# Norms whose second four outputs take x * g, with the memory's norm among the gate products

## The chip, the core and the metric

The kernel runs on one core of one Trainium2 chip. The time is that of one execution on the device, in microseconds (us). A core has a matrix engine (PE, which loads weights beside its matmuls as PEld), a vector engine (DVE), a scalar engine (ACT), a general engine (POOL), and queues that issue transfers (SP and others). Each engine runs its own instructions in order and waits on semaphores for the others.

## The reference, cut to what matters

Two blocks run one after the other on 256 rows of width 1024. The first mixes three branches (window attention, spatial gating, pooling), then attends to a memory, then has a feed-forward layer. The second puts 16 rows in front (272 in all), and has a recurrent mixer, a gated feed-forward layer with a convolution, an attention with stick-breaking weights, and a second such feed-forward layer. What the change touches:

```python
def rmsnorm(x, g):
    y = xf * lax.rsqrt(jnp.mean(xf * xf, axis=-1, keepdims=True) + EPS)
    return (y * g.astype(jnp.float32)).astype(x.dtype)
...
        h = rmsnorm(x, g_norm[l, 0])
        q, k, v, su, sv, pc, gate = split_columns(h @ w_in[l])
        ya = window_sink_attention(q, k, v, attn_sinks[l])
        yb = spatial_gating(su, sv, g_sgu[l], w_spatial[l], b_spatial[l])
        yc = multiscale_pool(pc, w_pool[l], pool_scale[l])
        proj = jnp.einsum('bsnc,ncd->bsnd', branches, w_branch[l])
        gates = jax.nn.sigmoid(gate.reshape(B, S, N_BRANCH, D_MODEL))
        merged = jnp.sum(gates * proj, axis=2)
        x = x + rmsnorm(merged @ w_out[l], g_norm[l, 1])
        hm = rmsnorm(x, g_norm[l, 2])
        mem_n = rmsnorm(mem, g_mem[l])
...
        hf = rmsnorm(x, g_norm[l, 4])
        yf = jnp.square(jax.nn.relu(hf @ w_up[l])) @ w_down[l]
...
        h = h + conv_glu_ffn(rms_norm(h, norm_ffn_g[layer]), ffn_up[layer], ffn_conv_w[layer],
                             ffn_conv_b[layer], ffn_down[layer])
```

Since 1 / rms is one number for each row of x, (x * g * r) @ w is the same as ((x * g) @ w) * r: a product can be started before r is known and scaled as it leaves PSUM.

## The kernel before

Activations lie feature-major: 128 partitions, 8 chunks of features (kc), and 256, 258 or 272 columns, one for each row of x. One output `ft` of a product is 128 features, summed over 8 kc in a PSUM bank. Each of these blocks is three matmuls (`mm3`): x and w are both split in a high and a low part (xh and xl, whi and wlo), and hi*hi, lo*hi and hi*lo are added up (lines 388, 389, 390). Weights come in groups of 8 blocks; ACT casts a group to whi, DVE subtracts wlo. A group listed in `W.whole` is used as it arrives, as one matmul of full width (L385, which the profile shows as two records), without cast and subtraction; it lies in a buffer of whi or wlo, which is why those names stand in its rows.

`Norm` prepares a product that begins with a norm. `steps` writes x * g (`raw`; named xh and xl, or xg in whole groups) and adds up squares in `acc`. `first` then computes the first four outputs from `raw`, chunk by chunk (`outer`: for each kc all four outputs), while a matmul with ones (L436, the colsum) and ACT give r = `rstd`. The first four leave PSUM through DVE (`ev` = ps * r). For the outputs behind them `split` makes `dst`, the normed x: nt = x * g * r on DVE, its high part xh on ACT, its low part xl on DVE. The second four (`then`) take `dst`, again chunk by chunk, and the ninth output and all others take it one output after the other (`dense`). Four norms have a second four: w_in (256 columns, split weights), w_up (256, whole), f_up0 (272, whole), f_up1 (258, split). WHOLE names the first group of w_up and of f_up0, and four groups from there are whole.

After w_in come 24 gate products (w_in 18 to 41), and after each of them three steps of side work: attention (eight blocks, each a chain of scores, reduces `am`, exponentials and scaling of `p`, transposes to `pT`, a product and the split to yah and yal), gating and pooling, by turns (`together`). Then the 24 branch products run in the order of outputs of n=1 and 2 by turns, then n=0 (which takes ya); `ev_merge` multiplies each with its gate on DVE and adds them up to `merged`, which w_out takes. Beside these products norm_mem makes `memn`, the normed memory. It has its buffer from h0 (the `dst` of w_in), so it can only write once the last gate product is done.

The order of the instructions on each engine is set as the program is built, by a scheduler that follows dependences and its own estimates, so a step given at another place in the code can land at another place on each engine.

Of the kernel before, what the change touches and what calls it, by code (L numbers as in the profile page):

```python
# [18 lines left out]
P = 128  # L19
# [245 lines left out]
def interleave(jobs, side, per=1):  # L265
    for job in jobs:
        job()
        for _ in range(per):
            next(side, None)
# [7 lines left out]
def together(*gens):  # L277
    gens = list(gens)
    while gens:
        for g in list(gens):  # L280
            try:
                next(g)
                yield
            except StopIteration:
                gens.remove(g)
# [3 lines left out]
def model(ctx: ExitStack, tc: tile.TileContext, a: dict, out: bass.AP, stage=None):  # L289
# [54 lines left out]
    W = Weights(nc.nc if WRAW else nc, a["wblk"], rawp, hlp, 2, 1)  # L344
    W.after = after
    for first in WHOLE:
        W.whole.update(range(first, first + 4))

    h = const.tile([P, KC, T], F32, name="h")
    vec = const.tile([P, NVEC], F32, name="vec")  # L350
# [61 lines left out]
    def xpair(n, k=KC, tag="x", bufs=2, pool=xp):  # L412
        xh = pool.tile([P, k, n], F32R, tag=tag + "h", name=tag + "h", bufs=bufs)
        xl = pool.tile([P, k, n], F32R, tag=tag + "l", name=tag + "l", bufs=bufs)
        return xh, xl
# [40 lines left out]
    class Norm:  # L456
# [33 lines left out]
        def first(self, items, then=(), ahead=None):  # L490
            def rstd():
                self.r = rstd_of(self.sums, self.n)

            assert not self.whole or len(W.order) // BLK_G in WHOLE
            tiles = outer([x[:2] for x in items], self.raw, self.n, 2, ahead, rstd)
            W.hold = []
            nc.stop()
            dst = xpair(self.n) if then else None
            for i, ((_, ft, ev), ps) in enumerate(zip(items, tiles)):
                if then:  # L500
                    self.split(dst, range(4 * i, 4 * i + 4) if i < 2 else ())
                    if i == 0:
                        table["hold"] += casts
                t = ep[0].tile([P, T], F32, tag="ev", name="ev")[:, :self.n]
                vtt(t, ps, self.r, op=ALU.mult)
                ev(ft, t)
            if then:
                for (_, ft, ev), ps in zip(then, outer([x[:2] for x in then], dst, self.n, 1)):
                    ev(ft, ps)
            return dst  # L510

        def split(self, dst, ks):
# [2 lines left out]
    def outer(items, x, n, nd=2, ahead=None, late=None):  # L515

        tiles = [(pd.tile([P, 512], F32, tag="pd", name="pd") if i < nd else pss.tile([P, 512], F32, tag="sc", name="sc"))[:, :n] for i in range(len(items))]
        for kc in range(KC):
            if ahead is not None:
                next(ahead)  # L520
            if kc == KC - 1 and late is not None:
                late()
            for (name, ft), ps in zip(items, tiles):
                mm3(ps, W.blocks([(name, kc, ft)]), x[0][:, kc, :], x[1][:, kc, :], kc == 0, kc == KC - 1)
        return tiles
# [16 lines left out]
    with tc.tile_pool(name="b1", bufs=1) as b1, tc.tile_pool(name="b2", bufs=2) as b2:  # L542
# [61 lines left out]
        def attention():  # L604
            ps = pss.tile([P, 2, 128], F32, tag="sc", name="sc")
            for i in range(2):
                nc.tensor.transpose(ps[:, i, :], vT[:, i * 128:(i + 1) * 128], ident)
            nc.scalar.copy(vtok, ps)
            yield
            for qt in (1, 0):  # L610
                nk = 128 * (qt + 1)
                for j in range(4):
                    sc = [pss.tile([P, 256], F32, tag="sc", name="sc")[:, :nk] for _ in range(2)]
                    mk = cmask[:, 128:384] if qt else cmask[:, 384:512]
                    for hh in range(2):
                        mm(sc[hh], lhsT=cmask[:, 0:128], rhs=mk, start=True, stop=False)
                    for hh in range(2):
                        r = slice(hh * 64, hh * 64 + 64)
                        mm(sc[hh], lhsT=qT[r, j, qt * 128:qt * 128 + 128], rhs=kT[r, 0:nk], start=False, stop=True)
                    yield  # L620
                    m = wk.tile([P, 4, 2], F32, tag="am", name="am")
                    for hh in range(2):
                        nc.vector.tensor_reduce(m[:, 0, hh:hh + 1], sc[hh], axis=AX.X, op=ALU.max)
                    vtt(m[:, 0, :], m[:, 0, :], sinks[:, j, :], op=ALU.max)
                    vts(m[:, 1, :], m[:, 0, :], -1.0, None, op0=ALU.mult)
                    vtt(m[:, 2, :], sinks[:, j, :], m[:, 0, :], op=ALU.subtract)
                    act(m[:, 2, :], m[:, 2, :], AF.Exp)
                    p = b2.tile([P, 2, 256], F32, tag="p", name="p")
                    for hh in range(2):
                        act(p[:, hh, :nk], sc[hh], AF.Exp, bias=m[:, 1, hh:hh + 1], accum_out=m[:, 3, hh:hh + 1])  # L630
                    vtt(m[:, 3, :], m[:, 3, :], m[:, 2, :], op=ALU.add)
                    nc.vector.reciprocal(m[:, 3, :], m[:, 3, :])
                    for hh in range(2):
                        vts(p[:, hh, :nk], p[:, hh, :nk], m[:, 3, hh:hh + 1], None, op0=ALU.mult)
                    yield
                    tp = pss.tile([P, 2, 2, 128], F32, tag="sc", name="sc")
                    for hh in range(2):
                        for kt in range(qt + 1):
                            nc.tensor.transpose(tp[:, hh, kt, :], p[:, hh, kt * 128:kt * 128 + 128], ident)
                    pT = b2.tile([P, 2, 2, 128], F32, tag="pT", name="pT")  # L640
                    nc.scalar.copy(pT[:, :, 0:qt + 1, :], tp[:, :, 0:qt + 1, :])
                    yield
                    o = pss.tile([P, 128], F32, tag="sc", name="sc")
                    for hh in range(2):
                        for kt in range(qt + 1):
                            mm(o[hh * 64:hh * 64 + 64, :], lhsT=vtok[:, kt, hh * 64:hh * 64 + 64], rhs=pT[:, hh, kt, :],
                               start=kt == 0, stop=kt == qt)
                    yield
                    ts_ = slice(qt * 128, qt * 128 + 128)
                    split(ya[0][:, j, ts_], ya[1][:, j, ts_], o)  # L650
                    yield
# [39 lines left out]
        def pooling():  # L691
            pool = b1.tile([P, 4, S], F32, name="pool")
            for g in range(4):
                src = cpad[:, g, :]
                for i in range(g + 1):
                    d = 1 << i
                    lo = 2 * d - 1
                    dst = b2.tile([P, 16 + S], F32, tag="psum", name="psum")
                    vtt(dst[:, lo:], src[:, lo:], src[:, lo - d:16 + S - d], op=ALU.add)
                    src = dst  # L700
                vtt(src[:, 16:32], src[:, 16:32], ptab[:, g, :], op=ALU.mult)
                stt(pool[:, g, :], src[:, 16:], 0.5 ** (g + 1), cpad[:, g, 16:], op0=ALU.mult, op1=ALU.subtract)
                yield
            for g in range(4):
                ps = pss.tile([P, S], F32, tag="sc", name="sc")
                mm(ps, lhsT=wpool[:, g, :], rhs=pool[:, g, :], start=True, stop=True)
                yield
                y = ep[0].tile([P, T], F32, tag="nt", name="nt")[:, :S]
                act(y, ps, AF.Copy, scale=vcol("pool_scale", g))
                split(yc[0][:, g, :], yc[1][:, g, :], y)  # L710
                yield

        nc.sync.dma_start(mem, a["memT"])
        jobs = [dense("w_in", 18 + i, KC, h0, S, ev_in) for i in range(24)]
        side = together(attention(), gating(), pooling())
        interleave(jobs, side, 3)
        drain(side)

        merged = xpair(S)
        memn = xpair(S)  # L720

        def norm_mem():
            acc = new_acc(S)
            for kc in range(KC):
                sumsq(mem[:, kc, :], acc, kc == 0, S)
            yield
            r = rstd_of([acc], S)
            for kc in range(KC):
                norm_split(lambda kc: mem[:, kc, :], "g_mem", 0, S, r, memn, (kc,))
                yield  # L730

        mg = {}

# [10 lines left out]
                    stt(merged[1][:, ft, :], mg[ft], 0.5, merged[0][:, ft, :], op0=ALU.mult, op1=ALU.subtract)  # L744
            return ev

        side = norm_mem()
        order = [(n, ft) for fts in (range(NBR), range(NBR, 8)) for ns in ((1, 2), (0,)) for ft in fts for n in ns]
        interleave([dense(f"w_br{n}", ft, 4, (ya, yb, yc)[n], S, ev_merge(n)) for n, ft in order], side)
        drain(side)  # L750

    def add_post(post, steps, width, stop, pool=(), ready=1, fill=0):

# [1086 lines left out]
```

## Time and profile before

| | us |
|---|---|
| median of 3 runs | 1325.83 |
| lowest and highest | 1320.94, 1328.16 |
| the profiled execution | 1322.63 |
| its span | 1320.9 |
| busy PE, DVE, ACT, POOL | 1268.0, 894.8, 705.6, 178.5 |

The span is the time from the first to the last instruction in the profile; the rest of the execution's own time lies around it. [...]

### The profile page before, as it was taken

The page shows a single profiled execution, that of the slowest core. Times are in us where ns is not written, and L with a number is a line of the kernel's source. Part 1 is how long each engine was busy: PE and PEld are TensorE (multiplying, and loading weights), DVE is VectorE, ACT ScalarE, POOL GpSimd, SP SyncE. Part 2 cuts the span into 40 slices and gives each one's busy share as a digit, 9 for nine tenths or more (in the row PEclk, how much of TensorE's full clock was granted, in tenths as well). Part 3 has the DMA queues.
Part 4 walks back from the last instruction along what each step waited for, and adds up shares of the span by engine and source line. Part 5 has one row for each costly group of instructions (what it writes and reads, how often), then busy time and mean ns, then how long its engine had stood idle before and what let it go on. Part 6 is the DMA issues. An engine that isn't in the chain of part 4 may idle for free.

```text
span 1320.9 us, 25715 instructions
## 1 busy us (share of the span) xinstructions
PE 1268.0 (96%) x10188; PEld 1176.1 (89%) x10188; DVE 894.8 (68%) x1812; ACT 705.6 (53%) x1349; POOL 178.5 (14%) x237
## 2 busy tenths in 40 slices
PE   5999998999999989999999999999999999899997
PEld 5999998888999976877877679999999989899997
DVE  6576586857664457567486468786567557989954
ACT  6566555675554434433242256665457666666643
POOL 1000000000000000434211002553000000135500
PEclk9999999998999999999999989999999999999999
DMA  7554455433555653432202125555554333655663
GB/s 257 157 175 134 155 149 162 153 128 128 178 190 179 188 192 120 128 96 65 71 13 64 50 65 166 170 176 178 175 170 142 125 95 87 191 171 178 191 182 106
DMA packets 54984, 188.16 MB, mean 142 GB/s; under 512 B 7598, under 2 KB 9792, under 8 KB 54736
## 3 DMA queue, kind: packets, MB, share of 16 engines
q1 hardware_dynamic: 53856, 185.27, 44.6%
q8 instruction: 80, 1.31, 0.4%
q0 software_dynamic: 464, 0.73, 0.3%
q10 hardware_dynamic: 544, 0.52, 0.1%
q14 instruction: 40, 0.33, 0.1%
HBM read 185.56 MB, written 1.05 MB: 141 GB/s over the span
## 4 chain that ended last, share of the span: by engine, by line
PE 84%; DVE 10%; ACT 3%; DMA 1%; issue 1%; POOL 1%; SPq 0%; DVEq 0%; ACTq 0%; POOLq 0%
PE pd L388 19%; PE pd L390 19%; PE pd L389 19%; PE pd L385 9%; PE l L986 3%; PE f L986 2%; DVE wlo L214 2%; PE sc L389 1%; PE sc L390 1%; PE sc L385 1%; DVE sh L214 1%; PE sc L388 1%; PE s L986 1%; DVE nt L214 1%; PE sc L1608 1%
## 5 line engine op out<-in xcount | busy, mean ns | idle before, releaser
L214 DVE TENSOR_TENSOR wlo<-raw,whi 128x1024 fp32r<-128x1024 f32 x270 | 332.5, 1233 | 208.6 <-ACT whi L214 204.1
L214 ACT CAST whi<-raw 128x1024 fp32r<-128x1024 f32 x298 | 312.2, 1049 | 299.4 <-PE pd L389 201.4
L388 PE MATMUL pd<-xh,whi 128*128 128x256 f32 (+2 forms) x1264 | 364.0, 289 | 18.9 <-ACT xh L214 12.4
L389 PE MATMUL pd<-xl,whi 128*128 128x256 f32 (+2 forms) x1264 | 361.2, 286 | 6.3 <-DVE xl L214 6.3
L390 PE MATMUL pd<-xh,wlo 128*128 128x256 f32 (+2 forms) x1264 | 361.0, 287 | 0.7 <-DVE wlo L214 0.6
L388 PEld LDWEIGHTS pd<-xh,whi 128*128 128x128 f32 x1264 | 241.8, 192 | 22.8 <-ACT xh L214 13.8
L389 PEld LDWEIGHTS pd<-xl,whi 128*128 128x128 f32 x1264 | 242.6, 192 | 7.4 <-DVE xl L214 7.2
L390 PEld LDWEIGHTS pd<-xh,wlo 128*128 128x128 f32 x1264 | 242.2, 192 | 1.6 <-DVE wlo L214 1.2
L389 PE MATMUL pd<-gl,whi 128*128 128x272 f32 (+1 forms) x352 | 100.1, 285 | 0.0
L388 PE MATMUL pd<-gh,whi 128*128 128x272 f32 (+1 forms) x352 | 100.0, 285 | 0.0
L390 PE MATMUL pd<-gh,wlo 128*128 128x272 f32 (+1 forms) x352 | 99.9, 284 | 0.0
L214 DVE SCALAR_TENSOR_TENSOR c<-pd,vec,c 128x256 f32<-128x256 f32 (+3 forms) x148 | 72.0, 487 | 13.6 <-ACT c L214 11.9
L214 POOL TENSOR_TENSOR wlo<-raw,whi 128x1024 fp32r<-128x1024 f32 x28 | 67.2, 2401 | 77.4 <-ACT whi L214 77.4
L390 PE MATMUL pd<-uh,wlo 128*128 128x256 f32 x256 | 72.5, 283 | 0.4 <-DVE wlo L214 0.4
L388 PE MATMUL pd<-uh,whi 128*128 128x256 f32 x256 | 72.6, 284 | 0.0
L389 PE MATMUL pd<-ul,whi 128*128 128x256 f32 x256 | 72.4, 283 | 0.0
L214 POOL TENSOR_TENSOR s<-s,c 128x272 f32<-128x272 f32 (+1 forms) x44 | 41.9, 953 | 191.3 <-ACT s L214 191.3
L390 PEld LDWEIGHTS pd<-gh,wlo 128*128 128x128 f32 x352 | 66.3, 188 | 0.0
L389 PEld LDWEIGHTS pd<-gl,whi 128*128 128x128 f32 x352 | 66.3, 188 | 0.0
L388 PEld LDWEIGHTS pd<-gh,whi 128*128 128x128 f32 x352 | 66.2, 188 | 0.0
L214 POOL MEMSET hn<- 128x8 f32 x1 | 0.1, 147 | 479.5 <-PE sc L436 479.5
L214 DVE TENSOR_TENSOR gl<-c,gh 128x272 fp32r<-128x272 f32 (+1 forms) x44 | 56.4, 1284 | 1.1 <-ACT gh L214 1.1
(443 smaller groups left out, 2650.8 us busy)
## 6 DMA issues: line engine op xcount, KB each, us to landing
raw<-in_wblk SPq DMA_DIRECT2D x298, 512.0 KB, 3.6
whi<-in_wblk SPq DMA_DIRECT2D x24, 512.0 KB, 3.5
wlo<-in_wblk SPq DMA_DIRECT2D x24, 512.0 KB, 3.6
mem<-in_memT SPq DMA_DIRECT2D x1, 1024.0 KB, 6.7
h<-in_xT SPq DMA_DIRECT2D x4, 128.0 KB, 5.5
h<-in_xT POOLq DMA_DIRECT2D x4, 128.0 KB, 6.5
out<-h SPq DMA_DIRECT2D x2, 256.0 KB, 2.4
out<-h ACTq DMA_DIRECT2D x2, 256.0 KB, 2.5
```

The costliest lines, as they stand in the source:

```text
L214: ins = f(*args, **kw)
L385: first = mm(ps, lhsT=wh, rhs=xh, start=start, stop=stop)
L388: first = mm(ps, lhsT=wh, rhs=xh, start=start, stop=False)
L389: mm(ps, lhsT=wh, rhs=xl, start=False, stop=False)
L390: W.used(mm(ps, lhsT=wl, rhs=xh, start=False, stop=stop))
L986: latest[:] = [nc.tensor.matmul(*args, **kw)]
L1608: mm(z[hh][:, c0:c0 + n], lhsT=k[j][r, s0:s0 + 128], rhs=q[j][r, q0 - Q0:], start=False, stop=True, skip_group_check=True)
```

## The change

Eight groups instead of four are whole at w_up and f_up0. In all four norms the second four outputs are computed one after the other from x * g, and leave PSUM through an `ev` on DVE as the first four do; only the ninth output and those behind it take `dst`. norm_mem follows gating in the side work of the gate products, and the branch products have no side work. `memn` is taken before `merged`, so it lies where x * g of w_in was.

```diff
     for first in WHOLE:
-        W.whole.update(range(first, first + 4))
+        W.whole.update(range(first, first + 8))
...
             dst = xpair(self.n) if then else None
+
+            def scaled(ft, ev, ps):
+                t = ep[0].tile([P, T], F32, tag="ev", name="ev")[:, :self.n]
+                vtt(t, ps, self.r, op=ALU.mult)
+                ev(ft, t)
+
             for i, ((_, ft, ev), ps) in enumerate(zip(items, tiles)):
...
-                t = ep[0].tile([P, T], F32, tag="ev", name="ev")[:, :self.n]
-                vtt(t, ps, self.r, op=ALU.mult)
-                ev(ft, t)
-            if then:
-                for (_, ft, ev), ps in zip(then, outer([x[:2] for x in then], dst, self.n, 1)):
-                    ev(ft, ps)
+                scaled(ft, ev, ps)
+            old = bank["dense"]
+            for i, (name, ft, ev) in enumerate(then):
+                if i in (1, 2):
+                    bank["dense"] = lambda: pss.tile([P, 512], F32, tag="sc", name="sc")
+                dense(name, ft, KC, self.raw, self.n, lambda ft, ps: scaled(ft, ev, ps))()
+                bank["dense"] = old
             return dst
...
         jobs = [dense("w_in", 18 + i, KC, h0, S, ev_in) for i in range(24)]
-        side = together(attention(), gating(), pooling())
-        interleave(jobs, side, 3)
-        drain(side)
-
-        merged = xpair(S)
         memn = xpair(S)
...
+        side = together(attention(), both(gating(), norm_mem()), pooling())
+        interleave(jobs, side, 3)
+        drain(side)
+
+        merged = xpair(S)
...
-        side = norm_mem()
         order = [(n, ft) for fts in (range(NBR), range(NBR, 8)) for ns in ((1, 2), (0,)) for ft in fts for n in ns]
-        interleave([dense(f"w_br{n}", ft, 4, (ya, yb, yc)[n], S, ev_merge(n)) for n, ft in order], side)
-        drain(side)
+        for n, ft in order:
+            dense(f"w_br{n}", ft, 4, (ya, yb, yc)[n], S, ev_merge(n))()
```

How instructions move, first on DVE at the norm of w_in. Before, from the eviction of the first four (`ev`) on, DVE has the rest of the split in one piece, with the subtractions of the next weights behind it (`acc` is the memory's sum of squares):

```order
L214 TENSOR_TENSOR wlo<-raw,whi 128x1024
L214 TENSOR_TENSOR xl<-nt,xh 128x256 x4
L214 TENSOR_TENSOR acc<-acc,sq 128x256
L214 SCALAR_TENSOR_TENSOR nt<-h,vec,rstd 128x256 x4
L214 TENSOR_TENSOR xl<-nt,xh 128x256 x4
L214 TENSOR_TENSOR wlo<-raw,whi 128x1024 x6
```

In the change the same place, from that `acc` on, reads:

```order
L214 TENSOR_TENSOR acc<-acc,sq 128x256
L214 TENSOR_TENSOR ev<-pd,rstd 128x256
L214 TENSOR_TENSOR ev<-sc,rstd 128x256
L214 SCALAR_TENSOR_TENSOR nt<-h,vec,rstd 128x256
L214 TENSOR_TENSOR wlo<-raw,whi 128x1024
L214 SCALAR_TENSOR_TENSOR nt<-h,vec,rstd 128x256 x3
L214 TENSOR_TENSOR ev<-sc,rstd 128x256
L214 TENSOR_TENSOR wlo<-raw,whi 128x1024
L214 TENSOR_TENSOR xl<-nt,xh 128x256
L214 TENSOR_TENSOR ev<-pd,rstd 128x256
L214 TENSOR_TENSOR wlo<-raw,whi 128x1024
L214 TENSOR_TENSOR xl<-nt,xh 128x256
```

Behind it come two reduces of the first attention block and the last two xl. So the second half of the split stands among evictions and subtractions. Next PE at w_up, from the colsum (`acc,ones` of 256 columns) on. Before, the second four take the normed x, chunk by chunk:

```order
L436 MATMUL sc<-acc,ones 128x256
L388 MATMUL pd<-xh,whi 128x256
L388 MATMUL sc<-xh,whi 128x256 x3
L436 MATMUL sc<-acc,ones 128x16
L389 MATMUL pd<-xl,whi 128x256
L390 MATMUL pd<-xh,wlo 128x256
```

In the change:

```order
L436 MATMUL sc<-acc,ones 128x256
L385 MATMUL pd<-xg,wlo 128x256 x2
L385 MATMUL sc<-xg,wlo 128x256 x2
L385 MATMUL pd<-xg,whi 128x256 x5
L385 MATMUL sc<-xg,wlo 128x256 x8
L385 MATMUL sc<-xg,whi 128x256 x8
L385 MATMUL pd<-xg,wlo 128x256 x8
L388 MATMUL pd<-xh,whi 128x256
```

The last row is the ninth output's first; the second four now stand ahead of every product of the split x. Last DVE at the end of the n=1 and 2 branch products. Before, the last attention block's scaling of p and its yal lie between merges (`gates`), and the first nt of the memory follows:

```order
L214 TENSOR_SCALAR p<-p,am 128x128 x2
L214 SCALAR_TENSOR_TENSOR gates<-gates,pd 128x256
L214 TENSOR_TENSOR wlo<-raw,whi 128x1024
L214 SCALAR_TENSOR_TENSOR gates<-gates,pd 128x256
L214 TENSOR_TENSOR gates<-gates 128x256
L214 TENSOR_TENSOR wlo<-raw,whi 128x1024
L214 TENSOR_TENSOR yal<-sc,yah 128x128
L214 SCALAR_TENSOR_TENSOR gates<-gates,pd 128x256 x2
L214 SCALAR_TENSOR_TENSOR nt<-mem,vec,rstd 128x256 x4
```

In the change the merges of n=1 and 2 end with the first two rows here, and the whole last block follows, from its reduces to its yal, ahead of the first merge of n=0:

```order
L214 TENSOR_TENSOR gates<-gates 128x256
L214 TENSOR_TENSOR wlo<-raw,whi 128x1024
L214 TENSOR_TENSOR yal<-sc,yah 128x128
L214 TENSOR_REDUCE am<-sc 128x1 x2
L214 TENSOR_TENSOR am<-am,sinks 128x2
L214 TENSOR_SCALAR am<-am 128x2
L214 TENSOR_TENSOR am<-sinks,am 128x2
L214 TENSOR_TENSOR am<-am 128x2
L214 RECIPROCAL am<-am 128x2
L214 TENSOR_SCALAR p<-p,am 128x128 x2
L214 TENSOR_TENSOR yal<-sc,yah 128x128
L214 SCALAR_TENSOR_TENSOR gates<-gates,pd 128x256 x2
```

On PE, 21 matmuls of n=0 products stand between this block's scores and its transposes, and nothing but its own product between these and the next n=0 rows. Over the whole program DVE has 8 subtractions of wlo fewer and 16 ev more, ACT 8 casts of whi fewer and two table loads more (15 instead of 13).

## Rows read from the trace of the kernel before

**Rows 1.** The page, its first part: busy time, share of the span, instructions.

```profile
PE 1268.0 (96%) x10188; PEld 1176.1 (89%) x10188; DVE 894.8 (68%) x1812; ACT 705.6 (53%) x1349; POOL 178.5 (14%) x237
```

**Rows 2.** Timeline of PE, first norm: start, length, instruction, count, idle time before and releaser.

```profile
25.30 0.28 PE L390 MATMUL sc<-xh,wlo 128*128 128x256 f32 x1
27.88 0.38 PE L388 MATMUL pd<-xh,whi 128*128 128x256 f32 x1 [2.31 <-ACT xh L214]
...
31.69 0.58 PE L389 MATMUL pd<-xl,whi 128*128 128x256 f32 x1 [3.07 <-DVE xl L214]
...
45.20 0.28 PE L388 MATMUL pd<-xh,whi 128*128 128x256 f32 x1
```

**Rows 3.** Windows: busy PE, PEld, DVE, ACT, POOL (instructions), clock, DMA share, GB/s.

```profile
32.00:37.00 5.00, 5.00 (x25) 5.00 (x25) 3.90 (x11) 2.45 (x5) 0.00 (x0) 0.50 0.31 105
60.00:80.00 20.00, 20.00 (x168) 19.92 (x167) 16.20 (x25) 11.22 (x17) 0.00 (x0) 1.00 0.60 184
100.00:140.00 40.00, 40.00 (x331) 38.02 (x331) 24.31 (x46) 26.83 (x57) 0.00 (x0) 1.00 0.46 137
194.00:212.00 18.00, 13.36 (x102) 12.17 (x100) 14.81 (x35) 7.82 (x16) 0.00 (x0) 1.00 0.36 117
307.00:313.00 6.00, 5.70 (x26) 5.59 (x27) 6.00 (x18) 3.72 (x9) 0.00 (x0) 0.50 0.04 17
786.00:790.00 4.00, 4.00 (x19) 4.00 (x20) 4.00 (x12) 1.96 (x5) 0.00 (x0) 0.50 0.38 131
1130.00:1149.00 19.00, 18.97 (x159) 18.76 (x157) 19.00 (x34) 14.33 (x25) 3.13 (x4) 1.00 0.56 168
```

**Rows 4.** Timeline of DVE, first norm.

```profile
25.69 1.23 DVE L214 TENSOR_TENSOR wlo<-raw,whi 128x1024 fp32r<-128x1024 f32 x1 [0.33 <-ACT whi L214]
26.84 1.67 DVE L214 SCALAR_TENSOR_TENSOR nt<-h,vec,rstd 128x256 f32<-128x256 f32 x4
28.42 0.75 DVE L214 TENSOR_TENSOR ev<-pd,rstd 128x256 f32<-128x256 f32 x2
...
34.48 1.43 DVE L214 TENSOR_TENSOR xl<-nt,xh 128x256 fp32r<-128x256 f32 x4
```

**Rows 5.** Timeline of PE, w_up.

```profile
289.02 1.13 PE L385 MATMUL pd<-xg,whi 128*128 128x256 f32 x4 [0.24 <-ACT xg L214]
...
302.93 0.59 PE L436 MATMUL sc<-acc,ones 128*128 128x256 f32 x2
305.50 0.39 PE L388 MATMUL pd<-xh,whi 128*128 128x256 f32 x1 [1.97 <-ACT xh L214]
...
321.54 0.28 PE L388 MATMUL pd<-xh,whi 128*128 128x256 f32 x1
```

**Rows 6.** Timeline of PE, f_up0.

```profile
780.75 1.08 PE L385 MATMUL sc<-xg,wlo 128*128 128x272 f32 x4
...
785.75 0.60 PE L389 MATMUL pd<-xl,whi 128*128 128x272 f32 x1 [2.90 <-DVE xl L214]
...
799.95 0.29 PE L388 MATMUL pd<-xh,whi 128*128 128x272 f32 x1
```

**Rows 7.** Timeline of PE, f_up1.

```profile
1152.53 0.36 PE L388 MATMUL pd<-xh,whi 128*128 128x258 f32 x1 [3.56 <-DVE c L214]
```

**Rows 8.** Waits of PE in 184 to 216: us in total, times, longest.

```profile
PE pd L388 <- DVE gates L214: 2.8, 4, 1.4
PE pd L388 <- ACT y L214: 1.2, 1, 1.2
```

**Rows 9.** Timeline of ACT, first norm.

```profile
28.96 1.28 ACT L214 ACT_TABLE_LOAD   x1
```

**Rows 10.** Timeline of DVE, the last attention block.

```profile
177.12 0.48 DVE L214 TENSOR_REDUCE am<-sc 128x1 f32<-128x128 f32 x2
...
182.41 0.48 DVE L214 TENSOR_SCALAR p<-p,am 128x128 f32<-128x128 f32 x2
...
188.49 0.29 DVE L214 TENSOR_TENSOR yal<-sc,yah 128x128 fp32r<-128x128 f32 x1 [1.84 <-ACT yah L214]
```

## The prediction

> **What bounds the kernel now.** I read the page first: the matrix engine (PE) is busy 96% of the span [rows 1], so only three things can move the time: work on PE, gaps on PE, and stretches in which PE runs at half its clock. The timeline of PE at the places where the change works, and the windows around them, then show where gaps and half clock are.
>
> At the first norm (w_in) the first four outputs end at 25.58 us (25.30 + 0.28). PE then waits 2.31 us for ACT's xh and, after four products, 3.07 us for DVE's xl, and the ninth output starts only at 45.20 [rows 2]. That is 19.6 us for 32 blocks. At full clock a split block is three matmuls at 20.00 / 168 = 0.119 us [rows 3], so 32 blocks need 11.4 us. [...] What PE waits for is the chain on DVE: nt from 26.84, the evictions, then xl until 35.9 [rows 4].
>
> The same happens at w_up: the colsum ends at 303.53 (302.93 + 0.59, two records), the second four start at 305.50, and the ninth output at 321.54 [rows 5]; the clock is 0.50 in 307 to 313 [rows 3]. And at f_up0: end at 781.83, a wait of 2.90 at 785.75, ninth output at 799.95 [rows 6], with 0.50 in 786 to 790 [rows 3]. At f_up1 there is no such wait: DVE is busy 19.00 of 19 us behind it, and PE loses 3.56 us later, at 1152.53, to a PSUM bank that DVE's c rows free [rows 3, 7].
>
> The branch products are the fifth place. In 194 to 212 PE is busy 13.36 of 18.00 us [rows 3]; of the 4.6 us lost, 2.8 go to DVE's merging of gates in four waits of at most 1.4, and 1.2 to ACT's y [rows 8]. There norm_mem's nt and xl stand in DVE's queue among the merges.
>
> **The change part by part.**
>
> *First norm.* The second four no longer need xh and xl of the normed x, so PE goes on at 25.58 without a wait: 32 blocks x 0.357 = 11.4 us, to 37.0. The weights are there in time: two of the four lo halves are subtracted by 26.9 [rows 4], and by DVE's order after the other two come near 30.1 and 31.8, for outputs that PE reaches at 31.3 and 34.2. Then come the transposes of v and the first attention scores (about 1.5 us of PE work, moved here from later), so the ninth output starts near 38.5. DVE does, from 26.84 on and by the order after: nt x4 (1.67), ev x4 (1.43), a sum (0.33), wlo (1.14), xl x4 with a wlo between (1.43 + 1.14), a sum, three ev, four nt, two wlo, and so on, at 0.33 per ev, sum and xl, 0.40 per nt and 1.14 per wlo. That puts the sixth xl at 41.4 and the last two at 43.0, behind two reduces of the attention. The ninth output wants them at 40.4 and 41.1: a new wait of some 1.9 us. It ends at 43.4, where before it ended at 45.20 + 2.86 = 48.1 without the 1.5 us of attention. Gain 48.1 + 1.5 - 43.4 = **6.2 us**. Bounds: no new wait gives 8.1; a wait with a spell of half clock like that of [rows 3] (5 us lose 2.5) gives 3.7.
>
> *w_up.* These groups are now raw too. A whole block takes (302.93 - 289.02) / 32 = 0.435 us [rows 5] against 0.357 for a split one, so 32 of them cost 2.5 us more PE, and run from 303.53 to 317.4. The ninth output starts there, not at 321.54: gain **4.1 us**. The last xl stands behind the eviction of the seventh output (PE done at 313.9) and its relu, so it lands near 315.2, ahead of need; four wlo and four whi go away, four ev come. Bounds: 3 (an xl or wlo late by a us) to 4.2.
>
> *f_up0.* At 272 columns a whole block is 0.435 x 272 / 256 = 0.462 us, an estimate from [rows 5]; 32 of them are 14.8 us, and the ninth output starts at 781.83 + 14.8 = 796.6 instead of 799.95 [rows 6]: gain **3.4 us** (2.5 to 3.6).
>
> *f_up1.* No gap to remove. DVE gets four ev, 4 x 0.33 = 1.3 us, in the stretch in which it is always busy, so the wait at 1152.53 can grow by that; against it, the four outputs free their banks after one DVE instruction instead of ACT's and two of DVE's. Ends -1.5 and +1; I take **-0.9**, nearer to the full row since DVE has no slack there [rows 3]. An ev from PSUM costs what the row shows: two in 0.75 us, one every 0.33 [rows 4]. [...]
>
> *norm_mem among the gates.* It leaves the branch stage and lands, by the order after, near 100 to 140 us. DVE gets 8 nt and 8 xl, 8 x (0.40 + 0.33) = 5.9 us; it has 40 - 24.3 = 15.7 us free there. ACT gets two table loads of 1.28 [rows 9] and 8 casts of about 0.4, 5.8 us, and has 13.2 free. PE is busy all 40 us [rows 3], with three banks for its outputs to lean on. Cost 0; were the cover gone, the two table loads would show, 2.6 us.
>
> *Branch stage.* DVE is busy 14.8 us in 194 to 212, PE 13.4 [rows 3]. Of the 5.9 us of norm_mem some 4 fall there, and without them DVE has less to do than PE. That gives back the 4.6 - 1.2 = 3.4 us of waits on DVE; the wait on y stays. But the side steps are now shared with norm_mem's, and the last attention block slips: its reduces stand behind all sixteen evictions of n=1,2, and its ya is wanted by every output of n=0. Its chain, added up from [rows 10] and the rows of the same block on ACT and PE between them (reduces 0.5, small steps 0.8, exps 0.9, scaling 0.5, transposes 0.5, copies and products 1.6), is 4.7 us; 21 matmuls (2.5 us) stand beside it. New wait 2.2 us, between 0 and 9.2 (the 11.7 us that the last block took before, from 177.12 to 188.78, less the 2.5). I take 2.2, since the rows of this block now stand one behind the other on DVE. Net **+1.2** (-6 to +3.4).
>
> **Sum.** 6.2 + 4.1 + 3.4 + 1.2 - 0.9 = 14.0 us. The profiled execution took 1322.63, so 1308.6; it lies 3.2 us under the median of the runs shown (1325.83), from which the same sum gives 1311.8. I say **1310**, which is a base of 1324 less 14; the times below are from that base.
>
> **Rivals.**
> (a) *The clock falls at the new waits.* The ninth output of w_in waits 1.9 us and the last attention block 2.2; in the rows, waits of 2.31 and of 1.97 were the start of a spell at 0.50, while the waits of up to 1.4 in the branch stage left the clock at 1.00 [rows 2, 3, 5, 8]. Each spell costs about 3 us: gain 8, time 1316. [...]
> (b) *The last attention block keeps its old pace*, 11.7 us: 9.2 us of idle PE instead of 2.2, gain 7, time 1317; with a spell at half clock 1320. For it: in the trace each block takes that long. Against it: there it shares its queues with weights and gates, here not.
> (c) *The wait only moves.* If DVE, with ev, nt, xl and wlo in one queue, delivers the last xl no earlier than the ninth output started before (45.2 in w_in, 321.5 at w_up, 800.0 at f_up0), nothing is gained, and every us beyond that is lost. With the four ev more at each of the four norms (1.3 us each, 5.3 in all), less 1.2 in the branch stage, that is 1328, slower than before. For it: DVE is solid in 26.84 to 35.9 already [rows 4]. Against it: by my reckoning the last xl comes at 43.0 and 315.2, near that point at w_in but far from it at w_up.
> (d) *All goes well*: no wait at the ninth output, none at the last block, 8.1 + 4.2 + 3.6 + 3.4 = 19 us, time 1305, and 1303 with a better f_up1 and the lower base.
>
> **Chances.** Forecast 0.55 (1305 to 1315), (a) 0.20, (b) 0.10, (c) 0.07, (d) 0.08. A difference of 0.5%, 6.6 us, is about what a measurement of this kernel tells from none; the bound of faster is 1319.2. All of the forecast and of (d), most of (a) and half of (b) lie under it: 0.85. Slower, above 1332.5, takes (c) with the last block at its old pace: 0.04. Same 0.11. The range 1303 to 1320 holds all but (c) and the tails of (b) and (d).
>
> **What would show it.** In the profile after, PE goes from the first four of w_in into the second four with no idle row, at clock 1.00, and the ninth output ends near 43.4 after a wait on xl of about 2 us; at w_up the L385 rows go on for 32 blocks at 0.435 us right behind the colsum, at f_up0 likewise; no window there shows 0.50. In the branch stage one wait of PE on yal or on a transpose of p takes the place of four waits on gates. The wait on c at f_up1 is 4 to 5 us. The number of table loads is 15. The prediction is wrong if windows at 0.50 remain behind these places, if the gate products show idle PE, or if PE waits over 5 us at the last attention block.

## The result, and the profile after

The changed kernel takes 1303.11 us (median of 4 runs, 1301.97 to 1304.20) against 1323.38 us (4 runs, 1317.15 to 1328.16). The ratio is 0.9848, 95% interval 0.9818 to 0.9877: 1.5% faster, 20.3 us. Forecast were 1310 us (1303 to 1320) and a gain of 14 us. Run again later beside other kernels, the same change took 1308.71 us (1302.90 to 1313.53) against 1323.86, a gain of 15.2 us; why the same program differs by 10 us is taken up below.

The profiled execution of the change took 1302.94 us, and its span is 1301.2. Its granted clock, which the profile gives as a share of PE's full speed, is 0.995 on the mean, against 0.988 before; in the clock records of both profiles it is 1.00 or 0.50, and a window that reads otherwise holds some of each. From the page, busy time of the engines, to be set beside [rows 1]:

```profile
PE 1264.0 (97%) x10124; PEld 1169.7 (90%) x10124; DVE 889.0 (68%) x1820; ACT 700.4 (54%) x1343; POOL 181.0 (14%) x237
```

The span is 19.7 us shorter, busy PE only 4.0. To see what PE's time consists of I took two things off each span: idle PE (the span less busy PE), and busy PE times (1 less the granted clock), added up over windows of 1 us, as an estimate of what half clock costs. The rest stands for work at full clock. The estimate counts a matmul at 0.50 as twice as long as one at 1.00. At w_up before, matmuls of 256 columns start every 0.213 us at 0.50 (21 of them from 308.50 to 312.98) and every 0.119 at 1.00, 1.8 times as far apart, so there it is about an eighth too high:

```profile
312.77 0.41 PE L390 MATMUL pd<-xh,wlo 128*128 128x256 f32 x1
312.98 0.41 PE L388 MATMUL sc<-xh,whi 128*128 128x256 f32 x1
...
313.62 0.28 PE L388 MATMUL sc<-xh,whi 128*128 128x256 f32 x1
313.74 0.28 PE L389 MATMUL sc<-xl,whi 128*128 128x256 f32 x1
```

| | span | idle PE | cost of half clock | work at full clock |
|---|---|---|---|---|
| before | 1320.9 | 52.9 | 12.1 | 1255.9 |
| the change | 1301.2 | 37.2 | 3.3 | 1260.7 |
| difference | -19.7 | -15.7 | -8.8 | +4.8 |

The +4.8 goes with 64 whole blocks in place of split ones, for which the prediction's block times make 2.5 + 2.7. It is no exact price: over the profiles of the experiments this work is 1259.2 to 1263.0 us with the whole blocks and, the kernel with filler left out, 1255.7 to 1257.0 without. So by this reckoning 24.5 us were taken off PE's waits and slow spells, and some 5 us paid back.

The places of [rows 2], [rows 5] and [rows 6] after the change. PE's timeline at w_in, with all rows from 24 to 48 us that show a wait or are not products of split weights:

```profile
36.32 0.38 PE L614 MATMUL sc<-ident,vT 128*128 128x128 f32 x2
36.64 0.39 PE L623 MATMUL sc<-cmask 2*128 2x256 bf16 x2
36.95 0.70 PE L626 MATMUL sc<-kT,qT 64*128 64x256 f32 x4
...
46.61 0.39 PE L388 MATMUL pd<-xh,whi 128*128 128x256 f32 x1 [0.17 <-ACT svu L214]
47.60 0.39 PE L390 MATMUL pd<-xh,wlo 128*128 128x256 f32 x1 [0.48 <-DVE wlo L214]
```

No wait on xh or xl is left. At w_up and f_up0 the whole blocks (L385) run straight into the ninth output:

```profile
304.15 3.62 PE L385 MATMUL pd<-xg,wlo 128*128 128x256 f32 x16
307.42 0.47 PE L388 MATMUL pd<-xh,whi 128*128 128x256 f32 x1
...
777.35 3.83 PE L385 MATMUL pd<-xg,wlo 128*128 128x272 f32 x16
780.82 0.49 PE L388 MATMUL pd<-xh,whi 128*128 128x272 f32 x1
```

Windows of the change at the same places, columns as in [rows 3]: the clock is 1.00 at all three norms, and 0.66 at one new place, 183 to 188, behind a window in which PE is busy 1.60 of 3 us. At f_up1 PE is busy 2.40 of 5 us, and the clock stays at 1.00:

```profile
24.00:36.00 12.00, 12.00 (x103) 12.00 (x102) 11.90 (x26) 10.24 (x20) 0.00 (x0) 1.00 0.55 175
180.00:183.00 3.00, 1.60 (x11) 0.92 (x10) 1.10 (x5) 0.75 (x4) 0.00 (x0) 1.00 0.36 146
183.00:188.00 5.00, 5.00 (x32) 5.00 (x31) 4.26 (x10) 2.87 (x5) 0.00 (x0) 0.66 0.07 18
294.00:309.00 15.00, 15.00 (x76) 13.37 (x75) 14.48 (x37) 10.12 (x26) 0.00 (x0) 1.00 0.23 70
766.00:781.00 15.00, 15.00 (x68) 12.43 (x66) 15.00 (x34) 10.47 (x19) 3.54 (x2) 1.00 0.22 71
1129.00:1134.00 5.00, 2.40 (x20) 2.23 (x19) 5.00 (x11) 3.86 (x7) 0.91 (x2) 1.00 0.62 175
```

The new place is the last attention block, as the waits of PE in 170 to 206 name it; the four waits on gates of [rows 8] are gone:

```profile
PE pd L388 <- ACT y L214: 1.0, 1, 1.0
PE sc L646 <- DVE p L214: 0.6, 1, 0.6
PE sc L653 <- ACT pT L214: 0.5, 1, 0.5
PE pd L388 <- ACT yah L214: 0.4, 1, 0.4
```

At f_up1 the wait of [rows 7] is still there, and shorter:

```profile
1133.69 0.36 PE L388 MATMUL pd<-xh,whi 128*128 128x258 f32 x1 [2.60 <-DVE c L214]
```

### The profile page after: what moved, and what is told of

Read it like the earlier page. It is cut to its first block, busy times and chain, and to the rows that moved or that the text cites. A ratio compares the mean times of both kernels' runs of the same rounds, so it can differ in the third digit from the quotient of the medians.

```text
span 1301.2 us, 25584 instructions
## 1 busy us (share of the span) xinstructions
PE 1264.0 (97%) x10124; PEld 1169.7 (90%) x10124; DVE 889.0 (68%) x1820; ACT 700.4 (54%) x1343; POOL 181.0 (14%) x237
## 4 chain that ended last, share of the span: by engine, by line
PE 88%; DVE 7%; ACT 2%; issue 1%; DMA 1%; POOL 1%; SPq 0%; DVEq 0%; POOLq 0%; ACTq 0%
PE pd L388 20%; PE pd L390 20%; PE pd L389 20%; PE pd L385 11%; PE l L993 3%; PE sc L385 2%; PE f L993 2%; DVE sh L214 1%; PE s L993 1%; DVE wlo L214 1%; PE sc L1615 1%; PE sc L1645 1%; PE p L993 1%; PE sc L389 1%; PE sc L388 1%
## 5 line engine op out<-in xcount | busy, mean ns | idle before, releaser
L214 ACT CAST whi<-raw 128x1024 fp32r<-128x1024 f32 x290 | 303.6, 1048 | 291.7 <-PE pd L389 194.2
L214 DVE TENSOR_TENSOR wlo<-raw,whi 128x1024 fp32r<-128x1024 f32 x262 | 323.8, 1237 | 191.4 <-ACT whi L214 190.1
L388 PE MATMUL pd<-xh,whi 128*128 128x256 f32 (+2 forms) x1264 | 361.6, 287 | 10.6 <-ACT xh L214 6.3
L390 PE MATMUL pd<-xh,wlo 128*128 128x256 f32 (+2 forms) x1264 | 358.7, 285 | 0.6 <-DVE wlo L214 0.5
L389 PE MATMUL pd<-xl,whi 128*128 128x256 f32 (+2 forms) x1264 | 358.5, 284 | 0.5 <-DVE xl L214 0.5
L388 PEld LDWEIGHTS pd<-xh,whi 128*128 128x128 f32 x1264 | 240.0, 190 | 12.9 <-ACT xh L214 6.6
L390 PEld LDWEIGHTS pd<-xh,wlo 128*128 128x128 f32 x1264 | 240.1, 190 | 1.9 <-DVE wlo L214 1.0
L389 PEld LDWEIGHTS pd<-xl,whi 128*128 128x128 f32 x1264 | 240.5, 190 | 1.4 <-DVE xl L214 0.7
L389 PE MATMUL pd<-gl,whi 128*128 128x272 f32 (+1 forms) x352 | 100.1, 285 | 0.0
L388 PE MATMUL pd<-gh,whi 128*128 128x272 f32 (+1 forms) x352 | 100.0, 285 | 0.0
L390 PE MATMUL pd<-gh,wlo 128*128 128x272 f32 (+1 forms) x352 | 99.9, 284 | 0.0
L214 DVE SCALAR_TENSOR_TENSOR c<-pd,vec,c 128x257 f32<-128x257 f32 (+3 forms) x144 | 70.0, 486 | 13.0 <-ACT c L214 11.3
L388 PE MATMUL pd<-uh,whi 128*128 128x256 f32 x256 | 72.6, 284 | 0.0
L389 PE MATMUL pd<-ul,whi 128*128 128x256 f32 x256 | 72.4, 283 | 0.0
L390 PE MATMUL pd<-uh,wlo 128*128 128x256 f32 x256 | 72.4, 283 | 0.0
L214 POOL TENSOR_TENSOR s<-s,c 128x272 f32<-128x272 f32 (+1 forms) x44 | 44.7, 1018 | 185.8 <-ACT s L214 185.8
L390 PEld LDWEIGHTS pd<-gh,wlo 128*128 128x128 f32 x352 | 66.4, 189 | 0.0
L389 PEld LDWEIGHTS pd<-gl,whi 128*128 128x128 f32 x352 | 66.3, 188 | 0.0
L388 PEld LDWEIGHTS pd<-gh,whi 128*128 128x128 f32 x352 | 66.2, 188 | 0.0
```

What stands on the lines that cost most here:

```text
L214: ins = f(*args, **kw)
L388: first = mm(ps, lhsT=wh, rhs=xh, start=start, stop=False)
L389: mm(ps, lhsT=wh, rhs=xl, start=False, stop=False)
L390: W.used(mm(ps, lhsT=wl, rhs=xh, start=False, stop=stop))
```

## Stage by stage, for all kernels

The stages run from one event of the trace to the next: the colsum of w_in, the last gate product's eviction, the first and the last product with ya, the first y of w_out, the first product with xg (w_up) and with uh (w_down), the last with LA (the recurrent mixer's output) and the first with gh (f_dn0), the last with yoh (the attention's output) and the last with gh. Stages between these that no experiment touches are left out. In us:

| | before | change | w_in only | whole only | f_up1 only | memory only |
|---|---|---|---|---|---|---|
| start, to the colsum | 23.6 | 22.5 | 22.7 | 22.2 | 21.8 | 23.1 |
| w_in and gates | 136.3 | 129.1 | 129.8 | 136.5 | 136.7 | 134.5 |
| ya products | 14.3 | 16.5 | 14.3 | 14.2 | 14.3 | 15.3 |
| from there to y | 12.7 | 9.4 | 12.7 | 12.8 | 12.7 | 9.6 |
| w_up | 101.7 | 97.3 | 101.8 | 97.3 | 101.5 | 100.6 |
| f_up0 | 138.0 | 134.9 | 136.9 | 134.9 | 138.0 | 136.8 |
| f_up1 | 194.9 | 194.4 | 196.0 | 195.9 | 192.8 | 196.1 |

Such a table tells more than the times: a stage that a kernel leaves alone should read as before, and where it doesn't, that is the size of what one execution differs from the next (1.1 at w_up, 1.2 at f_up0 and f_up1). Much of it is half clock: with w_in only, the spell at f_up0 costs 1.6 us instead of 2.9, and that at f_up1 3.1 instead of 1.7.

## The experiments

**One part alone, four times.** The first four kernels take one part of the change each. In `first`, norms not in NEW keep the old path:

```diff
+            if then and then[0][0] not in NEW:
+                for (_, ft, ev), ps in zip(then, outer([x[:2] for x in then], dst, self.n, 1)):
+                    ev(ft, ps)
+                return dst
             old = bank["dense"]
```

and a norm not in NEW has four whole groups again; norm_mem is beside the branch products again, except in the fourth.

> The kernel before, with only the second four of w_in taken from x * g. Theory A (each part takes away its own gap and its own spell at half clock): the span from the colsum of w_in to the last gate product is shorter by 6 to 7.5 us, no PE wait on xh or xl at 25 to 32, clock 1.00 there, and all stages behind as before; time 6 to 7 us under the kernel before. Theory B (the gains of the whole change are partly one execution's luck, or come from parts working together): 0 to 4 us.

Measured: 1314.10 us against 1322.12, ratio 0.9942 (0.9920 to 0.9964), 8.0 us faster. The stage is 129.8 instead of 136.3, no wait on xh or xl is left and the clock is 1.00 from 24 to 40. Theory A, for its own stage; of the time, 1.5 us more came off than the stage shows.

> The kernel before, with only the second four of w_up and f_up0 taken from x * g, in eight whole groups each. Theory A: w_up 4.1 to 4.4 us and f_up0 3.4 us shorter, 7.5 to 8 us in all, although 64 whole blocks cost PE 5 us more than split ones. Theory B: 3 us or less, the rest of the gain belonging to other parts.

Measured: 1314.90 us, ratio 0.9941 (0.9918 to 0.9964), 7.2 us faster; w_up 97.3 and f_up0 134.9, the same as in the whole change to 0.1 us. PE is busy 16.00 of 16 us around the second four of w_up. Theory A: the 0.08 us that a whole block costs more are outweighed.

> The kernel before, with only the second four of f_up1 taken from x * g. Theory A as predicted (DVE is full there and gets four ev more): 0.9 us slower, the wait on c grows from 3.6 to about 4.9. Theory C (banks of four outputs come free after one DVE instruction, and the shorter wait leaves the clock at 1.00): the wait on c falls to about 2.6, no window at 0.50 behind it, and the stage is 0.5 to 1.5 us shorter.

Measured: 1323.90 us, ratio 0.9993 (0.9975 to 1.0011): nothing that the times can tell. In the profile the wait on c is 2.4 instead of 3.6 and the stage 192.8 instead of 194.9, with no spell at 0.50. So the profile sides with theory C; the predicted loss of 0.9 is not there.

> The kernel before, with only norm_mem moved among the gate products. Theory A: gate products unchanged, the four waits on gates (2.8 us) and the one on wlo gone, a wait of 1.4 to 2.2 us at the last attention block in their place, perhaps with a spell at half clock of 3 us: 0 to 2 us faster. Theory D (the branch stage is bound by PE as soon as DVE is relieved, and the last block costs nothing): 3.4 us faster.

Measured: 1316.99 us, ratio 0.9949 (0.9931 to 0.9968), 5.1 us faster, more than either theory said. The branch stage explains 2.1 of it: 15.3 + 9.6 instead of 14.3 + 12.7. Its waits are the three of the last attention block again, 1.5 us in all, but here the clock stays at 1.00 behind them:

```profile
184.00:190.00 6.00, 4.60 (x35) 3.72 (x34) 2.70 (x14) 1.79 (x8) 0.00 (x0) 1.00 0.33 96
190.00:200.00 10.00, 9.95 (x85) 9.94 (x85) 10.00 (x24) 6.50 (x11) 0.00 (x0) 1.00 0.45 131
```

Another 1.2 us lie in the recurrent mixer (105.5 instead of 106.7), which the first of these kernels shows too. The rest of the 5.1 is open. The four medians' gains add up to 18.5 us (the third is -1.8); the whole change's is 20.3, and 15.2 in its second measurement. So the parts add up as far as these times can tell.

**Gaps filled, nothing else.** Is half clock the consequence of the gap, and what is it worth? In the kernel before:

```diff
             if then:
+                fill = dict(w_in=20, w_up=12, f_up0=13).get(then[0][0], 0)
+                if fill:
+                    warm(fill, *summed)
                 for (_, ft, ev), ps in zip(then
```

> The kernel before, nothing of the change, but with matmuls of ones on ones, whose result nobody reads, right behind the first four outputs: 20 at w_in (4.8 us at the pace of the warm matmuls in the trace), 12 at w_up, 13 at f_up0. They fill the time in which PE waits for xh and xl and should not delay it. Theory A (what the gap costs beyond itself is the spell at half clock that PE's idleness brings): no window at 0.50 at the three norms, the second four end 2.7, 3.2 and 2.9 us earlier, 8 to 9 us faster. Theory B (the slow second four have another cause, or the filler delays them): no change, or slower by up to 3 us.

Measured: 1315.24 us against 1323.86, ratio 0.9936 (0.9917 to 0.9954), 8.6 us faster, theory A. PE's timeline at w_in shows the filler, and what is left of the 3.07 us of wait in [rows 2]:

```profile
26.09 4.62 PE L534 MATMUL idle<-ones 128*128 128x128 f32 x40
...
32.36 0.39 PE L389 MATMUL pd<-xl,whi 128*128 128x256 f32 x1 [1.16 <-DVE xl L214]
```

and the windows, which stood at 0.50 in [rows 3]:

```profile
33.00:38.00 5.00, 5.00 (x44) 5.00 (x44) 4.80 (x11) 2.61 (x6) 0.00 (x0) 1.00 0.33 103
303.00:312.00 9.00, 8.17 (x68) 7.87 (x67) 9.00 (x24) 5.86 (x14) 0.00 (x0) 1.00 0.20 60
772.00:784.00 12.00, 11.49 (x81) 10.69 (x80) 9.19 (x22) 9.26 (x17) 0.00 (x0) 1.00 0.29 87
```

This kernel has 42.8 us idle and 3.3 at half clock. PE computes nothing useful in the 10.5 us of filler (4.62 + 2.84 + 3.06) and still waits for the same xl, yet the kernel gains: the spell at half clock is caused by the gap. At the three norms 8.8 us of half clock are gone (2.7 + 3.2 + 2.9), and the stages of the three norms are 6.3 us shorter together, since filler and the waits that are left take 2.4 us more than the gaps did. The other 2.3 us of the 8.6 lie in stages without filler. The other profiles bear the cause out: wherever one of these three norms keeps its old gap a spell at 0.50 follows, twelve times out of twelve, and where the gap is removed or filled none does, in twenty-four. The price varies: with the same three gaps, the profile of memory only lost 5.1 us there.

**The change without norm_mem's move.** The diff is the reverse of the last two pieces of the change.

> The change without its last part: norm_mem stays among the branch products. Theory A (the parts add up): the branch stage is again 27.0 us instead of 25.9, all else as in the change; 1 to 4 us slower than the change, 16 to 19 us faster than the kernel before. Theory B (norm_mem's move carries more than the branch stage, as the 0.9949 of it alone suggests): 5 us slower than the change.

Measured: 1310.19 us, ratio 0.9902 (0.9874 to 0.9930), 1.5 us above the change beside it (1308.71) and 7.1 above the change's first time. Its four runs and those of the change beside it overlap, so the times decide nothing here. The profile has the old branch stage, 14.2 + 12.8, and at w_in, w_up, f_up0 and f_up1 the stages of the change to within 0.7 us.

**The last attention block early.** What the new wait costs, and whether it can go:

```diff
-        interleave(jobs, side, 3)
+        interleave(jobs, side, 4)
```

> The change with four side steps behind each gate product instead of three, so that the last attention block is done under the branch products of n=1 and 2, as it was before the change. Theory A (the wait of 1.4 us for the last block's p, pT and yah, and the spell at half clock behind it, cost 3 us): the stage from the first to the last ya product is 14.3 us as before and not 16.5, 2 to 3 us faster than the change, 1300 us. Theory B (the wait only moves to y or to the merging of gates): the same as the change.

Measured: 1300.71 us (1299.88 to 1302.43), ratio 0.9834 (0.9809 to 0.9860). The ya products take 12.6 instead of 16.5 us, the step to y 9.6; the stage of w_in and the gates is 1.2 longer (130.3). Waits of PE in 170 to 205:

```profile
PE pd L388 <- ACT y L214: 1.2, 1, 1.2
PE pd L388 <- ACT yah L214: 0.4, 1, 0.4
```

Of the 3.7 us gained 2.5 stay (1.6 against the second profile of the change, which had no spell there). Theory A. This is the lowest median of the study; beside the next kernel it took 1303.61 us (1301.71 to 1304.73), ratio 0.9855 (0.9829 to 0.9880).

**The change again.**

> The change itself, run again beside the others. Theory A: 1303 us; idle PE some 38 us and under 4 us lost to half clock, since there is no long wait of PE left at the norms; the spell behind the last attention block may or may not be there. Theory B (the first profile of the change was a lucky execution): 5 us or more above it.

Measured: 1308.71 us, runs at 1302.90, 1306.46, 1310.95 and 1313.53, with granted clocks of 0.996, 0.996, 0.989 and 0.990. The time is that of theory B, 5.6 us above the first; the idle PE is nearly that of theory A. The profiled execution (clock 0.990, span 1311.8) has 39.3 us idle, 2 more than the first profile, but 11.3 us of half clock instead of 3.3. Most of it, 8.4 us, lies in the recurrent mixer, which the change doesn't touch. Windows there, first in this execution, then in the first profile of the change:

```profile
595.00:600.00 5.00, 4.20 (x62) 3.34 (x61) 3.92 (x10) 1.71 (x6) 2.41 (x4) 0.86 0.02 3
600.00:610.00 10.00, 10.00 (x65) 7.91 (x66) 2.92 (x11) 1.20 (x4) 2.00 (x5) 0.50 0.00 0
```

```profile
593.00:598.00 5.00, 4.20 (x67) 3.46 (x66) 4.05 (x12) 1.74 (x7) 2.20 (x4) 1.00 0.01 3
600.00:620.00 20.00, 19.62 (x152) 15.27 (x149) 18.33 (x82) 7.11 (x21) 7.82 (x13) 1.00 0.24 80
```

Instructions and order are the same, and so is what PE did before: short matmuls, 4.20 us busy in 5, and the same four waits in the 22 us ahead (1.2, 0.4, 0.3 and 0.2 us). One execution has half clock behind that, the other not, and the stage is 113.4 instead of 106.1 us; what decides it no run here shows. f_up1 adds 2.9 us more of it, behind a wait on c of 3.0 us, while the branch stage has none this time (15.6 + 9.4).

**The old second four at f_up1, on top of the early last block.**

> The last block early, as in the run of that name, but the second four of f_up1 taken from the normed x again, as before the change. Theory A (there DVE is full; four ev more cost 0.9 us, as predicted): 1 us faster than with the new f_up1. Theory C (the old order waits 3.6 us on c and always brings a spell at half clock behind it, of 1.7 to 3.1 us; the new one waits 2.6 to 3.0 and mostly none): the stage from the last yoh product to the last gh product is 195 to 196 us instead of 194, 1 to 2 us slower.

Measured: 1303.73 us (1302.77 to 1309.05), ratio 0.9867 (0.9841 to 0.9893); the same with the new f_up1, run beside it:

> The last block early, run again beside it, for the difference of the two on one chip and as a second profile: 1300 to 1303 us, no spell at half clock in the branch stage. Theory B (the four runs of the first time were lucky): runs at 1305 and above, as the change had in its second run, by a spell in the recurrent mixer.

1303.61 us, just above what was expected: the branch stage has no spell, but the recurrent mixer has 3.4 us of half clock, in the place that theory B named. The medians of the two kernels are equal, so neither price of the second four shows in the times. The profiles again differ as theory C says: PE's waits on c with the old second four (lines of that kernel stand one lower), then with the new:

```profile
PE pd L389 <- DVE c L215: 4.1, 2, 3.6
```

```profile
PE pd L388 <- DVE c L214: 3.0, 1, 3.0
```

and the stage is 197.3 against 195.4 us. In both a spell at half clock follows. Over all twelve profiles, the old second four waited 3.5 to 3.6 us in one piece and had a spell behind it each time (six profiles, stage 194.9 to 197.3); the new one waited 3.0 with a spell in two and 2.4 to 2.6 without one in four (stage 192.8 to 196.4).

## Why the prediction was right, and where its terms were off

The direction, the places and the mechanism were right: PE's gaps and half clock at three norms. The sum of 14.0 was 5.7 short of the profile's 19.7. That 1303.11 lies at the very low end of the range, under the 1305 to 1315 of the forecast and near the price of rival (d), of whose conditions one came true (no wait at the ninth output), is in part the luck of four executions at a clock of 0.995 to 0.997; the second measurement, with two of four at 0.989 and 0.990, gave 1308.71, in the middle of the forecast. Term by term, from the stage table:

| term | predicted | measured |
|---|---|---|
| first norm | 6.2 | 7.2 (alone 6.5) |
| w_up | 4.1 | 4.4 (alone 4.4) |
| f_up0 | 3.4 | 3.1 (alone 3.1) |
| branch stage | 1.2 | 1.1 |
| f_up1 | -0.9 | +0.5 (alone +2.1) |
| start, and what the change doesn't touch | 0 | 3.4 |

*First norm.* Before, 32 blocks took 19.6 us where 32 at 0.357 take 11.4; of the 8.2 between, 5.4 were idle PE (2.31 + 3.07), and the estimate puts 2.7 down to half clock. The step "a new wait of some 1.9 us" was wrong: there is no wait on xl, and what PE waits in this stage is 0.65 us, later, for an svu and a wlo. Without the wait the prediction's bound is 8.1, and 7.2 came. DVE came nearly as reckoned; this execution runs 1.1 us ahead of before, and its last two xl end at 41.3:

```profile
39.92 0.74 DVE L214 TENSOR_REDUCE am<-sc 128x1 f32<-128x256 f32 x2
40.59 0.75 DVE L214 TENSOR_TENSOR xl<-nt,xh 128x256 fp32r<-128x256 f32 x2
```

But PE did not wait there. In its rows the sixth chunk of the ninth output has hi*hi (L388) and hi*lo (L390), not lo*hi (L389), which wants the xl that ends at 40.0; the next row begins a chunk that has all three before that xl is there, so it must be one of the first five chunks, of the tenth output:

```profile
38.87 0.28 PE L388 MATMUL pd<-xh,whi 128*128 128x256 f32 x1
38.99 0.28 PE L390 MATMUL pd<-xh,wlo 128*128 128x256 f32 x1
39.11 0.28 PE L388 MATMUL pd<-xh,whi 128*128 128x256 f32 x1
39.23 0.28 PE L389 MATMUL pd<-xl,whi 128*128 128x256 f32 x1
```

The scheduler had put work whose operands were there ahead of the rest of the ninth output. I had reckoned as if one output were finished before the next is begun.

*w_up and f_up0* came out to 0.3 us, with the higher price of whole blocks in the sum (+4.8 against 5.2).

*Branch stage.* The net is right by luck, since two errors offset each other. The waits on DVE are gone, as reckoned, and the step to y is 3.3 us shorter. The new wait is 1.5 us in three pieces, where the sum had 2.2 in one. Behind it came the spell of rival (a), 1.7 us of half clock, which the sum had left out; with it the ya products took 16.5 us, 0.9 to 1.2 more than the 15.6 and 15.3 without it, and there the stage gained 2.1 us (norm_mem alone) and 2.0 (the change again). So that rival happened in one profile of three with this wait; at the ninth output there was no wait of that kind for it. At the three norms of before each gap was followed by 0.50 and lost another 2.7 to 3.2 us; a spell of that kind behind each of the two new waits, and with it 1316, was too strong a forecast for this change. Rival (b) didn't happen: the chain from the last block's reduces to its yal took 4.6 us, from 178.30 to 182.94, where 4.7 were added up.

*f_up1.* The step that failed is "DVE gets four ev, ... so the wait at 1152.53 can grow by that": it shrank from 3.56 to 2.60, where 4 to 5 us had been named as the sign. Which of the two reasons did it, banks that come free after one DVE instruction or four outputs that end one by one instead of together, wasn't separated. The spell behind the wait, 1.6 to 3.1 us with the old order, is gone in four of the six profiles with the new. The price of an ev from PSUM held: at w_in two of 256 columns took 0.75 us after the change as before it, and the stage at f_up1 became no longer (194.4 against 194.9 us).

*norm_mem among the gates* cost nothing that shows, with 15 table loads: the stage of w_in and the gates is 129.1 us with the move and 129.8 without it (w_in only, and the change without the move), and ya's first product comes 24.2 to 24.3 us after the last gate's eviction in both. *Start:* the first colsum comes between 21.6 and 24.2 us in the profiles, at 22.5 and at 24.0 in the two profiles of the change, so its 1.1 us are no effect of the edit. The remaining 2.3 us are small differences in the stages between (0.8 from the first xkvh product to the last yoh one, 0.6 in the recurrent mixer up to its last product with `blk`); what makes them wasn't tested.

## What to carry to other kernels

A gap on PE cost more here than its idle time: at the three norms the half clock that followed cost 5.1 to 8.8 us, by the estimate, in the profiles that have all three gaps, and filling the gaps with useless matmuls took 6.3 us off their stages without the change. A product that need not wait for its norm's scale was worth doing here even at a dearer form (0.435 against 0.357 us a block, and 7.2 us faster), as long as PE then ran through. And when side work is added to a shared rotation, look where its last step lands: here one more step for each product brought the last attention block back under cover.

## What the runs showed of the hardware

The same program takes different times, and the granted clock goes with them. The 43 runs of the kernel before that were made beside the experiments fall in two heaps, about 1317 to 1323 us at a clock of 0.988 to 0.993 and 1324.5 to 1327.3 at 0.983 to 0.985; the change has 1301.97 to 1306.5 at 0.995 to 0.997 and 1311 to 1313.5 at 0.989 to 0.990. For the change, which has a profile on each side, 8.0 of the 10.6 us between their spans are, by the estimate, spells at 0.50 that come in one execution and not in the other; the kernel before has one profile, and there the same reading rests on the clocks alone. Such spells came or stayed away after the same waits: 1.5 us in three pieces at the last attention block, and the short waits in the recurrent mixer, behind 5 us in which PE was busy 4.20 in both executions. And a gap of the same length is followed by spells of different cost: the wait of 3.5 to 3.6 us at f_up1 lost 1.6 to 1.7 us in three profiles and 2.8 to 3.1 in three others. So of two profiles one has to take idle PE and half clock apart before a difference of 2 or 3 us is given to an edit.
